# Loading the output-projection weights of quarters 1 to 3 later, and splitting the first quarter's attention rows pair by pair

## The chip, the core and the metric

The kernel runs on one core of a Trainium2 chip. The metric is the device time of one execution in microseconds, as the median of several runs; the profile comes from one execution, which has its own time.

Five engines work in parallel, each through its own queue, in order: PE (TensorE, matmuls), DVE (VectorE), ACT (ScalarE), POOL (GpSimd) and SP (SyncE, which here only issues DMA transfers). An instruction that waits holds up all behind it on its engine.

## The reference

One layer of a streaming encoder, on 2048 prompt rows and 32 sample rows of width 1024. Cut to what matters here:

```
h = rms_norm(x, g_norm1) * (1 + scale1) + shift1
q, k, v, z, xbc_raw, dt_raw = jnp.split(h @ w_in, SPLITS, axis=-1)
attn = stick_breaking(q, k, v)            # 8 heads of 64, weights from a running product of 1 - sigmoid
attn = rms_norm(attn.reshape(bsz, l, SB_WIDTH), g_attn_out)
ssm  = ssd_mixer(z, xbc_raw, dt_raw, ...) # 8 heads, chunked scan, normed
mixed = jnp.concatenate([attn, ssm], axis=-1) @ w_out
x = x + gate1 * mixed
h2 = rms_norm(x, g_norm2) * (1 + scale2) + shift2
ff = (jax.nn.silu(h2 @ w_gate) * (h2 @ w_up)) @ w_down
x = x + gate2 * ff
```

## The kernel before

All matmuls keep float32 accuracy by splitting each operand into a rounded high part and a low rest (`split`: ACT makes the high part, DVE or POOL the rest) and adding three products (`mm3`, L130 to L132). So every weight panel is loaded to a tile `wr` (1 MB), split to `wh` and `wl`, and used. `wr` has two buffers, `wh` and `wl` three each, shared by all weights.

The prompt is worked on in four quarters of 512 rows. Up to about 840 us of the profile the input projection and the state mixer run. Then come attention of quarter 0 (`attn`, a0, whole), and with it the state half of quarter 0's output projection (`Wout.ssm` of w0). `Wout.rows` loads the finished attention rows of a head pair from DRAM (`ao<-aoD`), splits them into `mH` and `mL` and sums their squares (`sq`, `t<-one,sq`); `Wout.run` does that for all four pairs, then the attention half of the product, the residual, the second norm (transposes `t<-xn`) and the store of the FFN's input. For w0 all of `run` is written behind the end of a0.

From then on two streams, written as Python generators, are mixed into one program by `merge`:

- Stream A: attention of quarters 1 to 3 with a window of near keys (`attn_w`, tiles `Kw`, `Vw`), then the far pass `far_keys` for the rows whose weight reaches past the window: seven chunks of 256 keys, each with 16 score matmuls (`fz`, from `Kf` tiles with two buffers), two sigmoids, a scan, two transposes (`t<-fb`) and 8 matmuls into `facc` (from `Vf`); and a tail in which, for quarters 1 to 3 in turn, the rows `aof` are loaded, corrected (`far`) and stored. After it come the projections (`project`) of quarters 1 and 2, of the sample, and of quarter 3. `Wout.pre` loads the state rows `mixT`, asks for the first w_out piece (`opiece`: a 1 MB load, four ACT and four DVE instructions, L114 and L115), the gate rows `gr` and the residual rows. Their pool lies where attention's tiles were, so `gr` is loaded after the far pass.
- Stream F: the FFN of the four quarters, 11 panels each. A panel is 24 gate matmuls (`pg`), 24 up (`pu`), 24 gate, 24 up, and 48 down (`py`): 144. `Pieces` asks for each panel's weights one ahead.

Each `yield n` says how long the piece just written is thought to take, in ns. `merge` writes pieces of F until they make up A's number times a ratio. F may not pass into quarter g+1 before A has finished the projection of quarter g (`yield ("need", g + 1)`, at 1536, 3120 and 4704 FFN matmuls).

What `merge` writes is not yet the order on the engines: at build time a scheduler goes through the written program, takes an instruction when by its own estimate its inputs and a buffer are there, and so can put an instruction ahead of others that were written before it. Buffers are granted in the written order. The order on each engine is fixed after that.

Of the kernel before, what the change touches and what calls it, by code (L numbers as in the profile page):

```python
# [35 lines left out]
def body(tc, nc, I, O):  # L36
    V, A, G, PE = nc.vector, nc.scalar, nc.gpsimd, nc.tensor
    ctx = ExitStack()
    with ctx:
# [15 lines left out]
        def store(dst, src):  # L55
            nc.sync.dma_start(dst, src)
# [30 lines left out]
        class Pieces:  # L87


            def __init__(self, thunks, look=1):  # L90
                self.t, self.q, self.look = list(thunks), [], look
# [5 lines left out]
            def get(self):  # L97
                self.fill(1)
                r = self.q.pop(0)
                self.fill(self.look)  # L100
                return r
# [138 lines left out]
        def sums(stat, sq, hp, n):  # L240
# [4 lines left out]
                PE.matmul(t[:m, b:b + 1], lhsT=sq[:, b * P:b * P + m], rhs=one1, start=True, stop=True)  # L245
            V.tensor_copy(stat[:m, hp, :nb], t[:m, :nb])

        def attn(g, at_, na=NA):

            aT, d1 = scan_tiles(at_, na)  # L250
            top = 2 * g + 1
            heads = {}

            todo = [(hd, kc) for hd in range(NH) for kc in range(top, -1, -1)]
            got = []

            def fetch():
                if not todo:
                    return
                hd, kc = todo.pop(0)  # L260
                hp, r0 = hd // 2, (hd % 2) * 64
                Q = None
                if kc == top:
                    Q = at_.tile([P, 512], F32R, tag="Q", name="Q", bufs=2)
                    for i in range(2):
                        load(Q[i * 64:(i + 1) * 64].bitcast(F32), QT[i, hp, r0:r0 + 64, g * 512:(g + 1) * 512])
                K = at_.tile([P, 2, 256], F32R, tag="K", name="K", bufs=3)
                c0 = kc * 256
                for i in range(2):
                    load(K[i * 64:(i + 1) * 64].bitcast(F32), KT[:, hp, r0:r0 + 64, c0:c0 + 256].rearrange("a p t -> p a t"))  # L270
                Vt = at_.tile([P, 2, P], F32R, tag="V", name="Vt", bufs=4)
                load(Vt.bitcast(F32), VS[c0:c0 + 256, hd].rearrange("(b p) a d -> p b (a d)", p=P))
                got.append((Q, K, Vt))

            def front(hd, kc):
                Q, K, Vt = got.pop(0)
                fetch()
                if kc == top:
                    heads[hd] = [Q, po.tile([P, 512], F32, tag="o", name="o")]
                Q = heads[hd][0]  # L280
                diag = kc - 2 * g
                ws = [None, None]
                for pr in (1, 0):
                    if diag == 1 and pr == 0:
                        continue
                    z = zps()
                    zv = z.rearrange("p (a b) -> p a b", a=2)
                    for i in range(2):
                        qb = pr * 2 + i
                        PE.matmul(zv[:, i, :], lhsT=Q[:, qb * P:(qb + 1) * P], rhs=K[:, 0, :], start=True, stop=False)  # L290
                        PE.matmul(zv[:, i, :], lhsT=Q[:, qb * P:(qb + 1) * P], rhs=K[:, 1, :], start=False, stop=True)
                    mask = ([[P, 2], [-1, 256]], P) if diag == pr else None
                    ws[pr] = scan(at_, aT, zv, 256, d1[pr], kc == 2 * g + pr, kc == 0, mask)
                    yield 450
                return ws, Vt

            def back(hd, kc, ws, Vt):
                o = heads[hd][1]
                r0 = (hd % 2) * 64
                diag = kc - 2 * g  # L300
                hl = []
                for kb in (1, 0):
                    q0 = max(diag * 2 + kb, 0) if diag >= 0 else 0
                    t = tps()
                    for qb in range(q0, 4):
                        PE.transpose(t[:, qb * P:(qb + 1) * P], ws[qb // 2][:, qb % 2, kb * P:(kb + 1) * P], ident)
                    hh = at_.tile([P, 512], F32R, tag="hh", name="hh", bufs=2)
                    ll = at_.tile([P, 512], F32R, tag="ll", name="ll", bufs=2)
                    c = slice(q0 * P, 512)
                    split(hh[:, c], ll[:, c], t[:, c])  # L310
                    hl.append((kb, c, hh, ll))
                    yield (4 - q0) * 109
                for kb, c, hh, ll in hl:
                    vv = Vt[:, kb, :]
                    PE.matmul(o[:, c], lhsT=vv, rhs=hh[:, c], start=(kc == top and kb == 1), stop=False, skip_group_check=True)
                    PE.matmul(o[:, c], lhsT=vv, rhs=ll[:, c], start=False, stop=(kc == 0 and kb == 0), skip_group_check=True)
                    yield (512 - c.start) / 1.2
                if kc == 0:
                    hp = hd // 2
                    if hd % 2 == 0:  # L320
                        heads["a"] = at_.tile([P, 512], F32, tag="ao", name="ao", bufs=1)
                    ao = heads["a"]
                    tmp = at_.tile([P, 512], F32, tag="P", name="otmp", bufs=2)[0:64]
                    A.activation(tmp, o[64:128, :], AF.Copy)
                    V.tensor_tensor(ao[r0:r0 + 64, :], o[0:64, :], tmp, op=ALU.add)
                    if hd % 2 == 1:
                        store(aoD[g, hp], ao)

            fetch()
            fetch()  # L330
            yield 3000
            pend = None
            for hd in range(NH):
                for kc in range(top, -1, -1):
                    ws, Vt = yield from front(hd, kc)
                    if pend is not None:
                        yield from back(*pend)
                    pend = (hd, kc, ws, Vt)
            yield from back(*pend)
# [377 lines left out]
        class Wout:  # L717


            def __init__(self, g, pool, psum):  # L720
                self.g, self.pool, self.psum = g, pool, psum
                self.t0, self.n, self.s = (g * 512, 512, 0) if g < NQ else (SEQ, DEC, 1)
                self.tb = blocks(self.n)

# [3 lines left out]
            def pre(self):  # L728

                s, t0 = self.s, self.t0  # L730
                mH, mL = mHL
                for i, t in enumerate((mH, mL if s == 0 else mH[:, :, DEC:])):
                    load(t[:, :, :self.n].bitcast(F32), mixT[i, :, :, t0:t0 + self.n].rearrange("k p t -> p k t"))
                self.pf = Pieces([lambda k=k, hf=hf, g=g: opiece(k, hf, g) for k, g in ((4, gsc), (0, gac)) for hf in range(2)])
                self.pf.fill(1)
                xsrc = I["x_prompt"][0, t0:t0 + self.n] if s == 0 else I["x_sample"][0]
                self.gr, self.x1 = [], {}
                for hf in range(2):
                    t = self.tile("gr", "gr")
                    load(t.rearrange("p (m c) -> p m c", m=4), modD[16 + hf * 4:20 + hf * 4, s].unsqueeze(0).to_broadcast([P, 4, P]))  # L740
                    self.gr.append(t)
                for b, c, m in self.tb:
                    x1 = self.tile("x1", "x1", nb=len(self.tb), w=D)
                    load(x1[:m], xsrc[c:c + m])
                    for hf in range(2):
                        self.x1[hf, b] = x1[:, hf * 512:(hf + 1) * 512]
# [27 lines left out]
            def rows(self):  # L774

                mH, mL = mHL
                if self.s == 0:
                    def get(hp):
                        ao = self.tile("ao", "ao")
                        load(ao, aoD[self.g, hp])  # L780
                        return ao

                    nxt = [get(0), get(1)]
                    yield 1500
                    for hp in range(4):
# [50 lines left out]
                    yield 450  # L836

            def run(self):
                yield from self.rows()
                nb, m0 = len(self.tb), self.tb[0][2]  # L840
                ra = sm.tile([P, 4], F32, tag="ra", name="ra", bufs=2)
                V.tensor_reduce(ra[:m0, :nb], stat[:m0, :, :nb].rearrange("p h b -> p b h"), axis=AX.X, op=ALU.add)
# [152 lines left out]
        def project(g, pool):  # L995
            w = Wout(g, pool, zps)
            w.pre()
            yield 3000
            yield from w.ssm()
            yield from w.run()  # L1000

# [597 lines left out]
        with ExitStack() as pb_:  # L1599
            mp = pb_.enter_context(tc.tile_pool(name="mp", bufs=1))  # L1600
            mHL, stat = mixed(mp)
            pw0 = ExitStack()
            w0 = Wout(0, pw0.enter_context(tc.tile_pool(name="wo0", bufs=1)), dense_ps)
            w0.pre()
            merge2(a0, w0.ssm(), R1)
            pa0.close()
            fc = px_.enter_context(tc.tile_pool(name="fc", bufs=1, side="right"))
            far_consts(fc)
# [28 lines left out]
            def streamF():  # L1637
                hT = load_h(0, fp, None)
                for g in range(NQ):
                    hT = yield from ffn(g, fp, late, hT)  # L1640

            merge(streamA(), streamF(), 1.55)


        fx = ctx.enter_context(tc.tile_pool(name="fx", bufs=1))
# [110 lines left out]
```

## Time and profile before

| | |
|---|---|
| median of 3 runs | 2942.09 us (2938.08 to 2947.04) |
| profiled execution, its time | 2940.34 us |
| its span, first to last instruction | 2938.4 us |
| PE busy | 2729.8 us, 93% of the span |
| DVE, ACT, POOL busy | 53%, 40%, 52% |
| granted PE clock, mean | 0.963 |

By stage, from the stretches of the same execution:

| stretch, us | what runs | PE busy, us | granted clock |
|---|---|---|---|
| 0 to 950 | input projection, state mixer, attention of quarter 0 | 846.95 of 950 | 0.96, then 0.83 |
| 950 to 1060 | end of quarter 0, its output projection | 72.94 of 110 | 0.75 |
| 1060 to 1300 | window attention with the FFN | 230.91 of 240 | 1.00 |
| 1300 to 1502 | far pass with the FFN, quarter 1's first products | 168.34 of 202 | 0.91 |
| 1502 to 2500 | projections with the FFN | 986.19 of 998 | 1.00 |
| 2500 to 2938.4 | the FFN's last part | 424.46 of 438.4 | 0.99 |

A busy PE is not always at its full pace, since matmuls overlap; the pace is read from the number of matmuls in a stretch. The granted clock is the share of full speed that PE was given.

### The profile page before, as it was taken

The numbers are of one execution on the slowest core, as the hardware profiler recorded it, in microseconds if no ns is written. First come the engines' busy times: TensorE is split into PE (matmuls) and PEld (weight loads), VectorE is DVE, ScalarE is ACT, GpSimd is POOL, SyncE is SP. The second block draws the span as 40 slices with busy tenths as digits, with TensorE's granted clock in tenths as the row PEclk, the third lists the DMA queues.
The fourth block names the chain that finished last, engine by engine and source line by source line (L and its number), as shares of the span: only waits on it lengthen the run. The fifth ranks groups of instructions, "written<-read, shape, count | busy, mean of one in ns | idle before, by whom it ended". The sixth has DMA issues, their size and how long they took to land.

```text
span 2938.4 us, 41844 instructions
## 1 busy us (share of the span) xinstructions
PE 2729.8 (93%) x15467; PEld 2334.2 (79%) x15467; DVE 1563.9 (53%) x2575; ACT 1186.0 (40%) x2533; POOL 1532.6 (52%) x1318
## 2 busy tenths in 40 slices
PE   6998998998978689998879999999999999999998
PEld 5988997896977578876667887777787788899997
DVE  6577586766568567874344534434434422333336
ACT  6466365555535455522224334333243422322221
POOL 4767566564654635743136655544564445544445
PEclk8999998999988789999989999999999999999999
DMA  8755653463467787837745744534733722422221
GB/s 266 219 171 153 202 177 114 119 182 106 131 175 237 193 225 196 208 116 213 199 165 180 258 135 137 152 122 155 236 127 106 230 88 92 154 87 87 86 87 66
DMA packets 415619, 466.54 MB, mean 159 GB/s; under 512 B 34191, under 2 KB 330991, under 8 KB 415406
## 3 DMA queue, kind: packets, MB, share of 16 engines
q1 hardware_dynamic: 414478, 463.61, 52.7%
q8 instruction: 124, 2.03, 0.3%
q14 instruction: 89, 0.73, 0.1%
q10 hardware_dynamic: 896, 0.14, 0.0%
q0 software_dynamic: 32, 0.03, 0.0%
HBM read 372.66 MB, written 91.04 MB: 158 GB/s over the span
## 4 chain that ended last, share of the span: by engine, by line
PE 57%; DVE 6%; DMA 5%; issue 3%; POOL 2%; ACT 2%; SPq 1%; DVEq 0%; ACTq 0%; POOLq 0%
PE pg L130 5%; PE pg L131 5%; PE pg L132 5%; PE pu L130 5%; PE pu L131 5%; PE pu L132 5%; PE py L130 5%; PE py L131 4%; PE py L132 4%; PE z L130 2%; PE z L131 2%; PE z L132 1%; PE d L131 1%; PE d L130 1%; PE d L132 1%
## 5 line engine op out<-in xcount | busy, mean ns | idle before, releaser
L60 POOL TENSOR_TENSOR wl<-wr,wh 128x512 fp32r<-128x512 f32 x752 | 1010.3, 1375 | 861.7 <-ACT wh L59 778.5
L59 ACT ACTIVATE wh<-wr 128x512 fp32r<-128x512 f32 x816 | 450.3, 620 | 512.3 <-PE py L132 128.4
L130 PE MATMUL d<-wh,hH 128*128 128x256 f32 (+2 forms) x1088 | 316.0, 291 | 18.8 <-ACT hH L59 10.9
L132 PE MATMUL d<-wh,hL 128*128 128x256 f32 (+2 forms) x1088 | 311.8, 287 | 6.7 <-POOL hL L60 6.7
L130 PE MATMUL pg<-h,wh 128*128 128x512 f32 (+1 forms) x880 | 311.3, 354 | 3.7 <-POOL aT L378 2.5
L130 PE MATMUL pu<-h,wh 128*128 128x512 f32 (+1 forms) x880 | 310.5, 353 | 1.2 <-DVE sg L952 1.2
L131 PE MATMUL d<-wl,hH 128*128 128x256 f32 (+2 forms) x1088 | 311.4, 286 | 0.0
L132 PE MATMUL pg<-h,wl 128*128 128x512 f32 (+1 forms) x880 | 310.7, 353 | 0.6 <-POOL wl L60 0.6
L131 PE MATMUL pg<-h,wh 128*128 128x512 f32 (+1 forms) x880 | 310.7, 353 | 0.0
L132 PE MATMUL pu<-h,wl 128*128 128x512 f32 (+1 forms) x880 | 310.5, 353 | 0.0
L131 PE MATMUL pu<-h,wh 128*128 128x512 f32 (+1 forms) x880 | 309.9, 352 | 0.0
L130 PE MATMUL py<-wh,aH 128*128 128x512 f32 x704 | 282.5, 401 | 7.0 <-DVE ya L983 5.0
L131 PE MATMUL py<-wl,aH 128*128 128x512 f32 x704 | 277.0, 394 | 0.0
L983 DVE TENSOR_TENSOR ya<-py,ya 128x512 f32<-128x512 f32 x288 | 190.4, 684 | 148.4 <-PE py L132 146.8
L132 PE MATMUL py<-wh,aL 128*128 128x512 f32 x704 | 265.8, 394 | 2.8 <-DVE aL L60 2.8
L952 DVE TENSOR_TENSOR sg<-pg,sg 128x512 f32<-128x512 f32 (+1 forms) x110 | 64.8, 589 | 336.8 <-ACT sg L951 336.8
L130 PEld LDWEIGHTS d<-wh,hH 128*128 128x128 f32 (+1 forms) x1088 | 207.7, 191 | 23.2 <-ACT hH L59 12.5
L132 PEld LDWEIGHTS d<-wh,hL 128*128 128x128 f32 (+1 forms) x1088 | 206.9, 190 | 8.0 <-POOL hL L60 7.2
L131 PEld LDWEIGHTS d<-wl,hH 128*128 128x128 f32 (+1 forms) x1088 | 207.3, 191 | 0.7
L130 PEld LDWEIGHTS pg<-h,wh 128*128 128x128 f32 x880 | 165.6, 188 | 28.5 <-POOL aT L378 2.7
L130 PEld LDWEIGHTS pu<-h,wh 128*128 128x128 f32 x880 | 165.5, 188 | 24.2 <-DVE sg L952 1.4
L132 PEld LDWEIGHTS pg<-h,wl 128*128 128x128 f32 x880 | 165.4, 188 | 24.1 <-POOL wl L60 1.1
(434 smaller groups left out, 5686.7 us busy)
## 6 DMA issues: line engine op xcount, KB each, us to landing
wr<-in_w_in SPq DMA_DIRECT2D x48, 1024.0 KB
wr<-in_w_gate SPq DMA_DIRECT2D x44, 1024.0 KB
wr<-in_w_up SPq DMA_DIRECT2D x44, 1024.0 KB
wr<-in_w_down SPq DMA_DIRECT2D x44, 1024.0 KB
wr<-in_w_ada SPq DMA_DIRECT2D x24, 1024.0 KB
wr<-in_w_out SPq DMA_DIRECT2D x20, 1024.0 KB
h2D<-hl SPq DMA_DIRECT2D x64, 256.0 KB
Kw<-KT SPq DMA_DIRECT2D x48, 320.0 KB
```

The source lines that it names most:

```text
L59: A.activation(h, src, AF.Copy)
L60: (eng or V).tensor_tensor(l, src, h.bitcast(F32), op=ALU.subtract)
L130: PE.matmul(out, lhsT=sh, rhs=mh, start=(i == 0), stop=False)
L131: PE.matmul(out, lhsT=sh, rhs=ml, start=False, stop=False)
L132: PE.matmul(out, lhsT=sl, rhs=mh, start=False, stop=(i == n - 1))
L952: V.tensor_tensor(sg[:, :n], pg[:, :n], sg[:, :n], op=ALU.mult)
L983: V.tensor_tensor(dst, ps[:r], dst, op=ALU.add)
```

## The change

Three edits.

1. `pre` asks for the first w_out piece only for quarter 0. For the others `project` asks for it after a yield of 3500, and the products follow after 4500 more; before it was 3000 in all.
2. For quarter 0, `rows` is written into the mix with a0: it waits until `attn` has stored a pair, loads that pair, splits it and sums its squares. `run` then skips `rows`.
3. The ratio of the two streams goes from 1.55 to 1.45. (It becomes 4.0 after quarter 1's projection, before and now.)

```
+        stored = []
...
                         store(aoD[g, hp], ao)
+                        stored.append(hp)
...
-            def __init__(self, g, pool, psum):
+            def __init__(self, g, pool, psum, alone=True):
...
-                self.pf.fill(1)
+                if self.g == 0:
+                    self.pf.fill(1)
...
+                    if self.g == 0 and not self.alone:
+                        for hp in range(4):
+                            while len(stored) <= hp:
+                                yield 200
+                            ao = get(hp)
+                            yield 1500
+                            split(mH[:, hp, :], mL[:, hp, :], ao)
+                            sq = self.tile("tm", "sq")
+                            A.activation(sq, ao, AF.Square)
+                            yield 500
+                            sums(stat, sq, hp, 512)
+                        return
...
             def run(self):
-                yield from self.rows()
+                if self.alone:
+                    yield from self.rows()
...
             w.pre()
-            yield 3000
+            yield 3500
+            w.pf.fill(1)
+            yield 4500
             yield from w.ssm()
...
-            merge2(a0, w0.ssm(), R1)
+            merge2(a0, chain(w0.ssm(), w0.rows()), R1)
...
-            merge(streamA(), streamF(), 1.55)
+            merge(streamA(), streamF(), 1.45)
```

What the scheduler makes of it, at three places. First ACT, around the splits of quarter 0's rows (`mH<-ao`) and their squares (`sq<-ao`); `wh<-wr` is the FFN's first weights, `hh<-t` and `otmp` belong to attention's last head pair. Before:

```order
L59 ACTIVATE mH<-ao 128x512 x2
L59 ACTIVATE wh<-wr 128x512
L789 ACTIVATE sq<-ao 128x512
L59 ACTIVATE wh<-wr 128x512 x2
L324 ACTIVATE otmp<-o 64x512
L59 ACTIVATE wh<-wr 128x512
L59 ACTIVATE hh<-t 128x256
L59 ACTIVATE mH<-ao 128x512
L789 ACTIVATE sq<-ao 128x512
```

Now:

```order
L59 ACTIVATE mH<-ao 128x512 x2
L59 ACTIVATE wh<-wr 128x512
L795 ACTIVATE sq<-ao 128x512
L59 ACTIVATE wh<-wr 128x512 x2
L326 ACTIVATE otmp<-o 64x512
L59 ACTIVATE wh<-wr 128x512
L59 ACTIVATE hh<-t 128x256
L59 ACTIVATE mH<-ao 128x512
L795 ACTIVATE sq<-ao 128x512
```

Only the lines of the code are others; the instructions and their order are the same.

Second PE, in the sixth of the seven far chunks, around its transposes. Before:

```order
L131 MATMUL py<-wl,aH 128x512
L132 MATMUL py<-wh,aL 128x512
L594 MATMUL t<-ident,fb 128x128 x2
L575 MATMUL fz<-Kf,Qz 128x256 x2
L130 MATMUL py<-wh,aH 128x512
L131 MATMUL py<-wl,aH 128x512
L132 MATMUL py<-wh,aL 128x512
```

Now:

```order
L605 MATMUL facc<-Vf,fl 128x512
L578 MATMUL fz<-Kf,Qz 128x256 x12
L597 MATMUL t<-ident,fb 128x128 x2
L578 MATMUL fz<-Kf,Qz 128x256 x2
L605 MATMUL facc<-Vf,fh 128x512 x2
L605 MATMUL facc<-Vf,fl 128x512 x2
L578 MATMUL fz<-Kf,Qz 128x256 x4
```

The down matmuls (`py`) that stood between the score matmuls are gone; twelve score matmuls, of which the last four belong to the seventh chunk, stand together ahead of the transposes.

Third SP, where the first two w_out loads stand among the key loads of the far pass (`Kf`, 112 in all). Before:

```order
L53 DMA Kf<-KT 64x2x256
L53 DMA wr<-in_w_out 128x4x512
L53 DMA Vf<-VS 128x512
L53 DMA Kf<-KT 64x2x256 x12
L53 DMA wr<-in_w_out 128x4x512
L53 DMA Vf<-VS 128x512 x2
L53 DMA Kf<-KT 64x2x256 x8
L53 DMA Vf<-VS 128x512 x2
L53 DMA Kf<-KT 64x2x256 x8
L53 DMA wr<-in_w_gate 128x8x256
```

Now:

```order
L53 DMA wr<-in_w_gate 128x8x256
L53 DMA Kf<-KT 64x2x256 x16
L53 DMA wr<-in_w_out 128x4x512
L53 DMA Vf<-VS 128x512 x2
L53 DMA Kf<-KT 64x2x256 x8
L53 DMA Vf<-VS 128x512 x2
L53 DMA Kf<-KT 64x2x256 x8
L53 DMA wr<-in_w_out 128x4x512
L53 DMA Vf<-VS 128x512 x2
```

The two loads stood after 68 and 80 key loads, and the gate panel after them; now they stand after 48 and 64, and the gate panel ahead of them.

More of the change, by code (lines that the diff above doesn't have):

```diff
@@ L717, in body @@
         class Wout:
-            def __init__(self, g, pool, psum):
-                self.g, self.pool, self.psum = g, pool, psum
+            def __init__(self, g, pool, psum, alone=True):
+                self.g, self.pool, self.psum, self.alone = g, pool, psum, alone
                 self.t0, self.n, self.s = (g * 512, 512, 0) if g < NQ else (SEQ, DEC, 1)
@@ L1602, in body @@
             pw0 = ExitStack()
-            w0 = Wout(0, pw0.enter_context(tc.tile_pool(name="wo0", bufs=1)), dense_ps)
+            w0 = Wout(0, pw0.enter_context(tc.tile_pool(name="wo0", bufs=1)), dense_ps, False)
             w0.pre()
-            merge2(a0, w0.ssm(), R1)
+            merge2(a0, chain(w0.ssm(), w0.rows()), R1)
             pa0.close()
```

## The prediction

> **What bounds the kernel now.** I read the page first (busy shares, slices, groups), then stretches of the span, then the order of time where PE is not full, then who waited for the tiles there.
>
> ```profile
> PE 2729.8 (93%) x15467; PEld 2334.2 (79%) x15467; DVE 1563.9 (53%) x2575; ACT 1186.0 (40%) x2533; POOL 1532.6 (52%) x1318
> PE   6998998998978689998879999999999999999998
> PEclk8999998999988789999989999999999999999999
> ```
>
> PE is the bound: 93% busy. A slice is 73.5 us; after the first, PE is at 6 or 7 only in the 12th (808 to 882 us, ahead of the change), the 14th (955 to 1028) and the 21st (1469 to 1543). The order of the work is fixed at build time and PE takes it in that order, so a change of order with the same matmuls costs or saves PE idle time and slow clock, nothing else.
>
> ```profile
> 950.00:1000.00 50.00, 36.58 (x168) 29.55 (x167) 32.45 (x42) 18.46 (x37) 31.03 (x34) 0.83 0.58 143
> 1060.00:1300.00 240.00, 230.91 (x1295) 196.59 (x1294) 191.89 (x288) 122.31 (x227) 141.48 (x138) 1.00 0.73 186
> 1300.00:1400.00 100.00, 91.32 (x424) 72.71 (x423) 40.77 (x65) 24.17 (x49) 37.11 (x28) 1.00 0.67 180
> 1450.00:1500.00 50.00, 31.01 (x93) 21.22 (x92) 19.84 (x34) 1.24 (x3) 2.54 (x3) 0.70 0.60 206
> 1500.00:1550.00 50.00, 50.00 (x230) 41.01 (x229) 24.27 (x35) 17.33 (x31) 23.91 (x19) 0.98 0.37 120
> 2400.00:2450.00 50.00, 50.00 (x216) 40.20 (x215) 16.62 (x25) 13.68 (x26) 26.14 (x20) 1.00 0.33 106
> ```
>
> (Stretch, then busy time and count of PE, PEld, DVE, ACT and POOL, granted clock, DMA share, GB/s.) Where only the FFN runs, PE is full, at 50/216 = 0.2315 us a matmul. The change touches two places where it is not: the first quarter's end (950 to 1050), and the far pass with the start of quarter 1's projection (1400 to 1500).
>
> **First quarter: nothing moves.** The code asks that pairs 0 to 2 be loaded and split during attention. The trace shows that this already happens.
>
> ```profile
> L59 ACT ACTIVATE mH<-ao x16: 613/632/633, 957.4 to 2146.0; 128x512 fp32r<-128x512 f32 x16
> L325 DVE TENSOR_TENSOR ao<-o,otmp x8: 655/680/684, 875.1 to 973.0; 64x512 f32<-64x512 f32 x8
> 973.71 0.33 SPq L56 DMA_DIRECT2D aoD<-ao  x1
> 976.25 0.33 SPq L53 DMA_DIRECT2D ao<-aoD  x1
> 979.78 0.80 PE L130 MATMUL d<-wh,mH 128*128 128x512 f32 x1 [5.33 <-ACT mH L59]
> ```
>
> The first split starts at 957.4, the last head's rows are made at 973.0: the scheduler had hoisted the loads out of the later code. The new build has the same instructions in the same order with the same waits on all five queues up to the first down panel of the FFN, beyond this stage (the first piece of order above shows ACT). The 5.33 us wait for the last pair's store and reload stays. Cost and gain: 0.
>
> **The far pass: the FFN stops one panel earlier.** All weight panels share three wh/wl buffers. Quarter 1's first two w_out pieces take two of them and keep them until its state products have run; these need the gate rows, which land only after the last store of the far pass.
>
> ```profile
> 1491.33 0.92 SPq L53 DMA_DIRECT2D gr<-modD  x2
> 1495.27 1.41 DVE L761 SCALAR_TENSOR_TENSOR tm<-z,rsS,gr 128x512 f32<-128x512 f32 x2 [6.14 <-DMA gr<-modD]
> 1496.08 0.79 PE L130 MATMUL z<-wh,mH 128*128 128x512 f32 x1 [8.00 <-DVE tm L761]
> 1504.58 2.57 ACT L114 ACTIVATE wh<-wr,cols 128x512 fp32r<-128x512 f32 x4 [36.69 <-PE z L132]
> ```
>
> Read upward: the third w_out piece waits 36.69 us for a buffer, until the products run (1496), after gr (1491 to 1495). So the FFN stops in both builds after the gate half-panel (24 matmuls) that follows those two pieces. Counting pg, pu and py in PE's order, 1176 stand ahead of the first far matmul before and 1032 now, one panel of 144 less. Between the 80th and the last of 112 fz matmuls there were 99, and to the first far matmul 123; now 2. The last two of seven chunks and the pass's tail run bare (second piece of order).
>
> What that stretch takes now:
>
> ```profile
> 1408.12 0.40 PE L575 MATMUL fz<-Kf,Qz 128*128 128x256 f32 x2
> 1448.91 0.39 ACT L580 ACTIVATE aT<-fz 128x256 f32<-128x256 f32 x1 [1.70 <-PE fz L575]
> 1449.20 0.38 ACT L581 ACTIVATE fb<-fz 128x256 f32<-128x256 f32 x1
> 1451.88 0.42 DVE L590 TENSOR_TENSOR fb<-fb,fP 128x256 f32<-128x256 f32 x1
> 1456.51 0.38 PE L594 MATMUL t<-ident,fb 128*128 128x128 f32 x2
> 1470.32 1.41 PE L642 MATMUL far<-S,OZ 128*128 128x512 f32 x4
> 1408.10:1470.30 62.20, 52.69 (x216) 40.79 (x215) 29.05 (x55) 12.70 (x26) 5.22 (x4) 0.90 0.71 205
> ```
>
> From the 80th fz (1408.12) to the first far (1470.32): 62.2 us, PE 52.7 busy. The 121 FFN matmuls that leave are worth 121 x 0.2315 = 28.0 us and run later, where PE is full. So the stretch must come down to 34.2 us to break even. What holds it up:
>
> ```profile
> 1415.49 5.35 SPq L53 DMA_DIRECT2D Kf<-KT  x8
> 1423.34 0.80 SPq L53 DMA_DIRECT2D Vf<-VS  x2
> 1447.04 0.69 PE L575 MATMUL fz<-Kf,Qz 128*128 128x256 f32 x2 [2.10 <-DMA Kf<-KT]
> 1447.00:1450.50 3.50, 3.08 (x9) 2.46 (x10) 1.16 (x2) 0.88 (x3) 3.50 (x4) 0.52 0.90 279
> ```
>
> - Two bare chunks. Each needs 16 Kf and 4 Vf issues from SP: 16 x 5.35/8 + 4 x 0.80/2 = 12.3 us. Its 24 matmuls take 5.6 us at 0.2315, twice that at half clock: less, so SP is the pace. Two chunks 24.6 us, and one landing wait of 2.10 us, because the up and down panels (1 MB each) stand in SP's queue just ahead: 26.7 us. Bounds: no wait, 24.6; a wait of 2.10 at each of the eight Kf tiles, 41.4. I take the lower part: a tile's issue outlasts its use on PE, and no panel load stands behind the sixth chunk.
> - The tail, last sigmoid to far: 1470.32 - 1448.91 = 21.4 us. Its transposes waited until 1456.51 behind gate matmuls, though fb was ready at 1452.30. Now 12 product matmuls stand there, in the bank that the sigmoids free at 1449.58; at the half clock seen after such gaps (0.52 in the row above, so 0.2315/0.52 = 0.445 us a matmul) they end at 1454.9, which saves 1.6 us: 19.8 us. Bounds: 17.2 if the transposes start at 1452.3, 21.4 if nothing is saved.
>
> Sum 26.7 + 19.8 = 46.5 us against 34.2: **+12.3 us**. Bounds 41.8 (+7.6) and 62.8 (+28.6); the upper needs every wait at its worst.
>
> The half clock came after a gap of only 2.10 us. The Trainium skill, TensorE: Matmul & The Clock Gate, "Why this matters for your kernels", says drops are avoided while idle gaps stay under about 3 us. By that rule the 12 products would run at full clock, 2.6 us shorter, and the sum would be +9.7. The row decides: I keep the half clock.
>
> **The other terms.** Ratio 1.55 to 1.45 in attention of quarters 1 to 3: 772 FFN matmuls stand ahead of the 16th fz now, 812 before. The 40 less are part of the 144. PE is 96% full there (230.91 of 240) and DVE 80%; taking 9.3 us of PE away brings DVE to 83%, still no bound: 0. From the far matmuls to the products: the same 24 far matmuls and the same store, load and gr chain, both times after 24 product matmuls: 0. The 36 products and 72 FFN matmuls that then follow fill PE as the 78 products did (50.00 of 50 in 1500 to 1550): 0. The weights' fill 3500 later and the 5000 more in all per projection spread quarters 2, 3 and the sample over more FFN work; quarter 2's last transposes stand after 2262 FFN matmuls, quarter 3's after 4002, ahead of 3120 and 4704, where the FFN first needs them: 0. One wait may go or come:
>
> ```profile
> 1600.87 0.77 PE L130 MATMUL z<-wh,mH 128*128 128x512 f32 x1 [2.38 <-DMA mH<-mixT]
>   DMA wr<-in_w_out: 2.8, 2
> ```
>
> Quarter 2's mH load was 2.38 us late; 126 FFN matmuls stand ahead of its first product now, so up to -2.4. ACT waited 2.8 us in all for w_out to land, in two places; I take 0 for both.
>
> Against the profiled execution, 2940.34 (span 2938.4): 2940.3 + 12.3 = **2952.6 us**. That execution lies 1.8 under the median of the runs, 2942.09; about 0.3% (8.8 us) is what this measurement can tell from no change.
>
> **Rivals.**
> - *Same*, 2948: the bare chunks keep the SP pace without landing waits and the tail starts early, +7.6. For it: the chain needs nothing from the FFN. Against: the two panel loads in SP's queue. 0.29.
> - *Faster*, 2932: the thinner mixture and the wider spacing let late operands come in time wherever PE now waits for them: 9.1 us in 1060 to 1300, 8.7 in 1300 to 1400, 2.4 at the mH load, 20.2 in all. All of it gone gives 12.3 - 20.2 = -7.9 on its own time, 9.7 under the median. It decides from 12.3 of the 20.2 on. For it: PE waits there for K, V and DVE results, not for other matmuls. Against: fewer matmuls also cover less. 0.13.
> - *Slower still*, 2960: the later fill. In the trace w_out cost ACT 2.8 us; four projections with a first piece late by as much as one such pair would add 8, and the sum is +20. Against it: 126 FFN matmuls, 29 us, stand ahead of quarter 2's first product. 0.08. The Trainium skill, DMA: Bandwidth & Descriptors, "Rules for kernel authors", states the rule behind it: issue a transfer early and wait for it late. The trace so far agrees little, 2.8 us in five projections.
> - My forecast, 0.50.
>
> With a part of *faster* that falls short: slower by over 0.3% 0.57; within 0.32; faster 0.11. The range takes in the *same* case, part of *faster* and most of the upper bound: 2936 to 2966; the likeliest case alone has 2948 to 2960.
>
> **What would show it.** Right: the far chunks 6 and 7 with no pg, pu or py between them, some 12 to 14 us apart, PE half idle and its clock at half for about 25 us ahead of the first far matmul; that matmul near 1450, the end some 12 us later. First quarter: same times to 1090 us. Wrong: chunks that follow each other in 8 to 9 us, or a first far matmul ahead of 1438; or attention (1060 to 1300) ending more than 12 us early for its number of matmuls.

## The result, and the profile after

| | before | changed |
|---|---|---|
| median | 2944.57 us | 2978.44 us (2976.16 to 2981.24) |
| ratio | | 1.0118, 95% interval 1.0095 to 1.0140 |
| profiled execution, span | 2938.4 us | 2979.5 us |

The change makes the kernel 34 us slower. The forecast was 12.3 us slower, 2952.6, with 2966 as the upper end: the direction was right, the size was not. Two places carry the loss. One is the far pass, which the prediction named and priced too low; the other lies 600 us later, and the prediction had it at nothing.

From the page of the changed kernel's profile, the busy line and the two lines of slices that the prediction showed of before:

```profile
PE 2740.9 (92%) x15467; PEld 2342.8 (79%) x15467; DVE 1543.0 (52%) x2575; ACT 1186.3 (40%) x2533; POOL 1532.1 (51%) x1318
PE   7998998998978599998599999999799999999998
PEclk8999998999988799999699999999899999999999
```

As many matmuls as before. A slice is 74.5 us. The 20th (1415 to 1490) has fallen to 5 tenths with a clock of 6; before, the dip there was the 21st, a 7 with a clock of 8. And the 29th (2086 to 2160) shows a 7 with a clock of 8 where before there were only nines.

The stretches that the prediction showed of before, now of the changed kernel, and two new ones: the bare stretch from the 80th fz to the first far matmul, and the new dip.

```profile
950.00:1000.00 50.00, 36.56 (x168) 29.54 (x167) 32.41 (x44) 18.14 (x37) 30.98 (x34) 0.83 0.55 142
1060.00:1300.00 240.00, 230.04 (x1285) 196.05 (x1284) 191.28 (x289) 122.82 (x228) 144.98 (x138) 0.99 0.72 187
1300.00:1400.00 100.00, 95.53 (x446) 76.85 (x445) 39.43 (x72) 24.75 (x48) 25.84 (x20) 1.00 0.72 195
1450.00:1500.00 50.00, 31.39 (x92) 20.47 (x91) 19.23 (x33) 2.83 (x6) 6.58 (x6) 0.71 0.50 179
1500.00:1550.00 50.00, 50.00 (x229) 40.80 (x227) 17.92 (x28) 16.18 (x28) 24.57 (x19) 1.00 0.37 116
1403.00:1463.60 60.60, 33.42 (x90) 22.55 (x91) 13.39 (x32) 3.87 (x11) 0.00 (x0) 0.58 0.54 145
2105.00:2145.00 40.00, 19.95 (x78) 15.54 (x79) 10.62 (x17) 7.64 (x20) 15.33 (x14) 0.79 0.87 302
```

(Stretch, then busy time and count of PE, PEld, DVE, ACT and POOL, granted clock, DMA share, GB/s.) The first five are close to those of before (in the third PE does 22 matmuls more). In the sixth PE runs 90 matmuls in 60.6 us at a clock of 0.58. In the last it is busy half the time; the kernel before, in the same 40 us:

```profile
2105.00:2145.00 40.00, 39.92 (x180) 32.11 (x179) 19.54 (x25) 15.18 (x27) 28.00 (x22) 1.00 0.53 184
```

**The far pass.** The changed kernel's order of time on PE and SP, the two bare chunks (Kf and Vf are the key and value tiles, two buffers each):

```profile
1402.87 0.48 PE L578 MATMUL fz<-Kf,Qz 128*128 128x256 f32 x2 [1.76 <-DMA Kf<-KT]
1413.37 1.88 SPq L53 DMA_DIRECT2D Kf<-KT  x3
1417.10 0.79 PE L605 MATMUL facc<-Vf,fh 128*128 128x512 f32 x1 [3.79 <-DMA Vf<-VS]
1418.35 1.45 SPq L53 DMA_DIRECT2D Vf<-VS  x2
1419.85 11.57 SPq L53 DMA_DIRECT2D Kf<-KT  x15
1424.65 0.77 PE L578 MATMUL fz<-Kf,Qz 128*128 128x256 f32 x2 [4.36 <-DMA Kf<-KT]
1444.74 0.77 PE L578 MATMUL fz<-Kf,Qz 128*128 128x256 f32 x2 [3.20 <-DMA Kf<-KT]
1463.61 0.63 PE L645 MATMUL far<-S,OZ 128*128 128x512 f32 x2
```

Read with the waits: at 1415.25 SP comes to a Vf load whose buffer is still in use. PE frees it only after 1417.10, since it waited 3.79 us itself for the Vf before. SP goes on at 1418.35, the K loads behind go out from 1419.85, and PE waits 4.36 us for them. From the 80th fz (the second of the pair at 1402.87) to the last (1445.09, the second of the pair at 1444.74) it is 42.0 us; the tail to the first far matmul takes another 18.5. What SP waited for in these 43 us (in total, times, longest):

```profile
SPq L53 <- PE facc L605: 7.3, 7, 2.2
SPq L53 <- DMA Kf<-KT: 6.6, 3, 3.5
```

The first row is V buffers that PE freed late; the second the profile puts down to landings of K loads. The two chunks in the kernel before, and now:

```profile
1408.00:1449.00 41.00, 35.01 (x156) 27.56 (x155) 18.43 (x35) 10.88 (x22) 3.26 (x3) 0.94 0.86 243
1403.00:1446.00 43.00, 19.96 (x56) 13.11 (x56) 5.41 (x16) 3.03 (x9) 0.00 (x0) 0.56 0.68 180
```

Before, the 80th to the last fz took 40.2 us with 99 FFN matmuls in between. Those are gone, and the chunks have not become shorter.

**The seam of the FFN's quarters 1 and 2.** Here quarter 1's last panel brings its residual (ya, xf) in, and the sample's projection ends. The changed kernel, in order of time:

```profile
2108.45 0.54 POOL L150 TENSOR_TENSOR rsd<-rs,mhalf 32x1 f32<-32x1 f32 x1 [3.27 <-DVE rs L149]
2110.71 0.68 PE L841 MATMUL t<-ident,xn 32*128 32x32 f32 x8
2111.24 2.26 ACT L847 ACTIVATE hx<-t,mods,A 128x32 f32<-128x32 f32 x8 [5.31 <-PE t L841]
2113.55 2.22 ACT L59 ACTIVATE wh<-wr 128x512 fp32r<-128x512 f32 x4
2114.29 6.22 POOL L60 TENSOR_TENSOR wl<-wr,wh 128x512 fp32r<-128x512 f32 x5 [5.30 <-ACT wh L59]
2120.48 1.25 POOL L941 TENSOR_TENSOR ya<-ya,xf 128x512 f32<-128x512 f32 x1
2121.76 1.74 DVE L1004 TENSOR_TENSOR ya<-ya,yt 128x512 f32<-128x512 f32 x1 [4.83 <-POOL ya L941]
2124.35 0.79 PE L130 MATMUL pg<-h,wh 128*128 128x512 f32 x1 [12.96 <-DVE yt L1003]
2143.16 0.80 PE L130 MATMUL pg<-h,wh 128*128 128x512 f32 x1 [5.71 <-DVE yt L1003]
```

A chain through five in-order queues: the sample's norm (rsd on POOL, xn on DVE, transposes t on PE, hx on ACT); ACT stands 5.31 us for the transposes with weight splits behind; POOL stands 5.30 us for those splits, with the residual's addition behind; DVE stands 4.83 us for that, with the product yt behind, which empties the accumulator bank that PE writes next; and PE stands 12.96 us for that bank.

### The profile page after: what moved, and what is told of

It is laid out like the page before. It is cut to its first block, busy times and chain, and to the rows that moved or that the text cites. A ratio compares the mean times of both kernels' runs of the same rounds, so it can differ in the third digit from the quotient of the medians.

```text
span 2979.5 us, 41835 instructions
## 1 busy us (share of the span) xinstructions
PE 2740.9 (92%) x15467; PEld 2342.8 (79%) x15467; DVE 1543.0 (52%) x2575; ACT 1186.3 (40%) x2533; POOL 1532.1 (51%) x1318
## 4 chain that ended last, share of the span: by engine, by line
PE 60%; DVE 5%; DMA 5%; POOL 2%; issue 2%; ACT 1%; SPq 1%; DVEq 0%; ACTq 0%; POOLq 0%
PE pg L130 5%; PE pg L131 5%; PE pg L132 5%; PE pu L130 5%; PE pu L132 5%; PE pu L131 5%; PE py L130 5%; PE py L131 5%; PE py L132 5%; PE z L130 2%; PE z L131 2%; PE z L132 1%; DMA Vf<-VS 1%; PE d L131 1%; PE d L130 1%
## 5 line engine op out<-in xcount | busy, mean ns | idle before, releaser
L974 DVE TENSOR_TENSOR sg<-pu,sg 128x512 f32<-128x512 f32 (+1 forms) x110 | 65.0, 591 | 253.8 <-PE pu L132 252.8
L767 POOL TENSOR_TENSOR x<-x,tm 128x512 f32<-128x512 f32 (+1 forms) x68 | 96.2, 1419 | 180.3 <-DMA x<-in_x_prompt 118.4
```

Of the source, the lines that this page charges most:

```text
L767: G.tensor_tensor(x1[:m], x1[:m], tm[:m], op=ALU.add)
L974: V.tensor_tensor(sg[:, :n], pu[:, :n], sg[:, :n], op=ALU.mult)
```

## The experiments

A profiled execution can lie some us off its program's median: 7 above it for rows_only (2951.74), 8 for far_covered_2 (2960.47), 4 below it for the kernel before (2940.34). So each run is also read by its two places. All programs have the same matmuls. Each matmul was counted at the spacing it has where PE is full, and the times at which two programs had done the same amount were compared. "Far" is what a program lost on the kernel before between before's 1240 and 1545 us, "seam" between 2049 and 2339 us; both from one execution, and uncertain by some 3 us, by the spacing that is taken. "FFN ahead" counts FFN matmuls ahead of the first far matmul and, behind the stroke, those after the 80th fz; "sample" is where its last transposes stand.

| kernel | FFN ahead | sample | far, us | seam, us | ratio to before, interval |
|---|---|---|---|---|---|
| changed | 1032/2 | 3168 | 25.6 | 19.4 | 1.0118 (1.0095 to 1.0140) |
| ratio_only | 1032/2 | 2976 | 24.4 | -4.0 | 1.0052 (1.0034 to 1.0069) |
| late_weights_only | 1176/123 | 3240 | 1.0 | 7.4 | 1.0022 (1.0008 to 1.0036) |
| rows_only | 1176/123 | 3105 | 4.0 | 0.8 | 0.9994 (0.9980 to 1.0008) |
| sample_soon | 1032/2 | 3096 | 27.1 | 4.5 | 1.0076 (1.0047 to 1.0105) |
| yields_145 | 1032/2 | 3168 | 28.6 | 18.6 | 1.0143 (1.0122 to 1.0163) |
| late_fill_145 | 1032/2 | 2976 | 27.9 | -5.1 | 1.0062 (1.0040 to 1.0085) |
| panel_back | 1152/122 | 2905 | 5.9 | -4.5 | 0.9969 (0.9957 to 0.9982) |
| far_covered | 1266/213 | 2982 | -9.5 | -6.1 | 0.9999 (0.9987 to 1.0011) |
| all_sample_early | 1032/2 | 2832 | 33.4 | 1.3 | 1.0096 (1.0071 to 1.0121) |
| all_panel_back | 1176/146 | 3168 to 3194 | -3.2 | 3.8 | 1.0024 (1.0013 to 1.0035) |
| all_both_mended | 1176/146 | 2905 | 0.3 | -1.2 | 0.9956 (0.9939 to 0.9973) |
| far_covered_2 | 1266/213 | 2832 | -3.9 | 3.6 | 1.0026 (1.0010 to 1.0042) |
| vf_other_queue | 1032/0 | 2976 | 12.4 | -4.8 | 1.0032 (1.0016 to 1.0049) |
| residual_dve | 1032/2 | 3168 | 27.1 | -1.2 | 1.0075 (1.0045 to 1.0105) |
| best_vf | 1176/144 | 2905 | -4.1 | -0.2 | 0.9960 (0.9945 to 0.9975) |

**ratio_only**, the third edit alone.

```
-            merge(streamA(), streamF(), 1.55)
+            merge(streamA(), streamF(), 1.45)
```

> Before with the third edit alone (ratio 1.45). The changed kernel lost time at two places: 20 us by the end of the far pass, and 20 more at the seam of the FFN's quarters 1 and 2 (2105 to 2145 us), where a gate matmul waited 12.96 and then 5.71 us. Theory, two stalls with two causes: the ratio makes the first. 1032 FFN matmuls stand ahead of the first far matmul here, as in the changed kernel, and the sample's last transposes stand after 2976 of them, well ahead of the seam at 3120. So 18 to 22 us slower than before, some 2965 us, all of it between 1400 and 1510, and no PE wait over 3 us at the seam. Rival, one cause: the seam's stall follows from the panel that is missing, since all later FFN work then stands otherwise against the projections: 35 to 41 slower, some 2980. By the step of the prediction (bare stretch 46.5 us) it would be 12 slower, 2957.

2959.87 us, 16 slower. Far pass and seam, of this kernel:

```profile
1405.50:1464.30 58.80, 33.23 (x91) 22.82 (x91) 14.30 (x35) 3.87 (x11) 0.00 (x0) 0.57 0.50 141
2095.00:2160.00 65.00, 65.00 (x289) 52.73 (x288) 32.81 (x42) 22.10 (x39) 45.76 (x33) 1.00 0.71 240
```

The bare stretch is that of the changed kernel, and PE is full at the seam. The ratio alone makes the first loss and not the second.

**late_weights_only**, the first edit alone.

```
             w.pre()
-            yield 3000
+            yield 3500
+            w.pf.fill(1)
+            yield 4500
```

(and in pre, fill(1) for quarter 0 alone.)

> Before with the first edit alone (first w_out piece asked for after a yield of 3500, products after 4500 more; ratio 1.55). The order of the far pass on PE is that of before (1176 FFN matmuls ahead of the first far matmul, 123 behind the 80th fz); the sample's last transposes stand after 3240 FFN matmuls instead of 3105, behind the seam at 3120. Theory, two causes: no loss in the far pass, 15 to 22 us lost at the seam; some 2962 us. Rival, one cause (the panel): no loss, 2945 us within 9. Rival, late weights themselves: waits of ACT for in_w_out ahead of each of four projections, some 3 us each, spread over 1500 to 2400 us and not at the seam.

2950.00 us: 6 slower, and where the theory had it, but less than its 15 to 22. With the sample at 3240 the seam cost 7.4 us.

**sample_soon**, the whole change with the sample's yields cut.

```
-            yield 3500
+            k = 3 / 8 if g == NQ else 1
+            yield 3500 * k
             w.pf.fill(1)
-            yield 4500
+            yield 4500 * k
```

> The changed kernel with the sample's two yields cut to 3/8 (1312 and 1688, 3000 in all, as before); quarters 1 to 3 keep 3500 and 4500. The sample's last transposes stand after 3096 FFN matmuls, ahead of the seam, instead of 3168. Theory, two causes: the seam's stall goes, the far pass stays 20 us slower; some 2962 us. Rival (the seam's stall comes from the missing panel, or from quarter 2's or 3's later weights): nothing changes, 2978 us.

2966.70 us, 12 less than the change and near the theory's 2962. At the seam 4.5 us are left, with one wait of 2.81.

**rows_only**, the second edit alone (code as in the change).

> Before with the second edit alone (the first quarter's rows inside its attention). Every engine has the order of before up to the FFN's first down panel. Theory: same as before, 2945 us within 9, with the same 5.3 us wait of PE for the last pair's split. Rival (the edit lets the last pair come earlier or holds up an engine ahead of it): a change of more than 9 us, seen between 950 and 1060 us.

2944.28 us against 2943.85: nothing, as expected.

**yields_145** and **late_fill_145** part the first edit's halves, both at the ratio 1.45: the longer yield with the early load, and the late load with the old 3000 in all.

```
yields_145:     -            yield 3000
                +            yield 8000
late_fill_145:  -            yield 3000
                +            yield 1300
                +            w.pf.fill(1)
                +            yield 1700
```

(late_fill_145, and the programs below with a yield of 10000 or 20000 that start from the kernel before, also have the line in pre.)

> Before with the ratio 1.45 and a yield of 8000 ahead of each projection's products, but the first w_out piece asked for at once, as before. The sample's last transposes stand after 3168 FFN matmuls, as in the changed kernel. The ratio alone gave +16 us (1.0052), the whole change +34 (1.0118). Theory: it is the longer yield that pushes the sample's end onto the seam of quarters 1 and 2, so this is as slow as the whole change, some 2976 us, with a PE wait of over 8 us on yt near 2110. Rival (the later asking for w_out costs the rest): 2960 us, no such wait.

> Before with the ratio 1.45 and the first w_out piece asked for after a yield of 1300, the products after 1700 more (3000 in all, as before). PE's order is that of the ratio alone, with the sample's last transposes after 2976 FFN matmuls. Theory: asking later costs nothing, so as the ratio alone, some 2960 us, and no long wait at the seam. Rival (the later asking costs the rest): some 2972 us, with ACT waiting for in_w_out.

2984.39 and 2960.71 us, both as the theory had it. The longer yield makes the second loss; asking for the weights later costs nothing (1.0062 beside 1.0052 for the ratio alone, the intervals overlap; no wait of ACT for w_out shows in late_fill_145). Of yields_145 at the seam:

```profile
2128.43 0.79 PE L130 MATMUL pg<-h,wh 128*128 128x512 f32 x1 [12.95 <-DVE yt L986]
2095.00:2160.00 65.00, 45.42 (x181) 35.00 (x180) 30.07 (x41) 18.00 (x39) 27.86 (x22) 0.84 0.82 284
```

**panel_back** gives the far pass its panel again at the ratio 1.45: F gets written ahead of quarter 1's first w_out piece, so its panel gets the buffers.

```
-            yield 3000
+            yield 10000 if g == 1 else 1300
+            w.pf.fill(1)
+            yield 1700
...
-                        yield ("ratio", 4.0)
+                        yield ("ratio", 3.6)
...
-            merge(streamA(), streamF(), 1.55)
+            merge(streamA(), streamF(), 1.45)
```

> The ratio 1.45 in attention, but quarter 1 asks for its first w_out piece only after a yield of 10000, so that an FFN panel's weights get their buffers ahead of it: 1152 FFN matmuls stand ahead of the first far matmul (1032 with the ratio alone, 1176 before), 122 of them behind the 80th fz (2; 123). Quarter 1's last transposes stand after 1428, the sample's after 2905 (a ratio of 3.6 instead of 4.0 behind quarter 1). Theory: the far pass loses only for want of those matmuls, so the time is that of before, 2944 us within 9, and PE waits in 1400 to 1465 are those of before. Rival (the ratio costs 15 us in other ways: less FFN in attention, operands later): some 2958 us.

2935.48 us: the far loss shrinks from 24 to 6, and the whole is 9 us faster than before. So the lost panel, not the ratio as such, is what the far pass paid for.

**far_covered**: as panel_back, but with the ratio 1.55 kept and the yield 20000 in place of 10000.

> Ratio 1.55 as before, quarter 1's first w_out piece asked for after 20000: 1266 FFN matmuls ahead of the first far matmul, 213 of them behind the 80th fz, and 66 more among the far matmuls. The sample's last transposes stand after 2982 (ratio 3.6 behind quarter 1). Quarter 1's projection ends later, its last transposes after 1584 FFN matmuls, just as quarter 0 of the FFN ends. Theory (PE loses time in the far pass for want of FFN matmuls): of the 17 us that PE is idle in 1440 to 1485 in the kernel before, and the half clock beside them, some 10 to 15 us go; up to 10 may come back where the FFN's quarter 1 must wait for the projection; some 2936 us. Rival (the far pass is bound by its loads, which the FFN's weights delay): no gain there, 2944 to 2955.

2944.54 us, no gain. In the far pass the theory was right: PE is busy 96.07 of 110 us there, and was 85.01 before.

```profile
1400.00:1510.00 110.00, 96.07 (x417) 75.79 (x416) 48.00 (x83) 22.14 (x43) 20.82 (x16) 0.94 0.66 198
1653.88 0.80 PE L130 MATMUL pg<-h,wh 128*128 128x512 f32 x1 [18.40 <-DMA h<-h2D]
```

But quarter 1's projection ended after 1584 FFN matmuls, and at the seam of quarters 0 and 1 PE waited 18.40 us (and 3.71 more) for its result.

**all_sample_early**, **all_panel_back**, **all_both_mended** keep all three edits and mend one place, the other, or both.

```
all_sample_early:  -                        yield ("ratio", 4.0)
                   +                        yield ("ratio", 3.2)
all_panel_back:    -            yield 3500
                   +            yield 10000 if g == 1 else 3500
all_both_mended:   both
```

> The whole change, with the ratio behind quarter 1's projection 3.2 instead of 4.0; no yield is touched. The sample's last transposes stand after 2832 FFN matmuls instead of 3168, the far pass is that of the change (1032 ahead of the first far matmul). Theory (where the sample's end falls against the seam at 3120 sets the second stall, and nothing else): no wait over 3 us near the seam, the far pass as slow as in the change, so about 16 us slower than before, 2961 us. Rival (the longer yields cost by themselves, wherever the sample ends): 2975 to 2980.

> The whole change, but quarter 1 asks for its first w_out piece after 10000 instead of 3500: 1176 FFN matmuls ahead of the first far matmul, 146 of them behind the 80th fz. The sample's last transposes stay behind the seam, after 3168 to 3194. Theory (two causes that add up): the far pass loses nothing now, the seam's stall stays: 12 to 20 us slower than before, some 2960 us. Rival (the seam's stall needs the missing panel): as before, 2945.

> The whole change with both mends: quarter 1's first w_out piece after 10000, ratio 3.2 behind quarter 1. 1176 FFN matmuls ahead of the first far matmul, the sample's last transposes after 2905. Theory (the two places are the whole loss): the time of before or a few us less, 2935 to 2948. Rival (something else in the change costs too): 2955 or more.

2972.19, 2949.55 and 2928.77 us. The seam of all_sample_early is clean (1.3 us) with the long yields kept, so place decides there; but the total fell by 6 us and not 17, because its "far" is 33.4, with the same order on PE. Seven programs with these bare chunks have 24.4 to 33.4 us there. Of the 8 us that this one loses beyond the change only 2 lie in the two chunks (44.1 us for 42.0); it already waited longer for V and K tiles ahead of them (3.51 us at 1341.81, where the change waited 1.58 at 1337.09). Why is open. all_panel_back lost nothing in the far pass and only 3.8 us at the seam, and 9.0 ahead of it, with a wait of 6.32 us at the transposes of the sample's rows (the profile names a weight load that was issued just ahead of those rows): less than expected. With both mended the kernel is 13 us faster than before by the ratio, 0.9956 (15 by the medians), and some 50 faster than the change. Neither place has a gain to show (0.3 and -1.2), so the lead arises elsewhere; that was not followed. Its two places:

```profile
1400.00:1510.00 110.00, 85.99 (x326) 64.97 (x325) 46.80 (x80) 15.97 (x32) 13.86 (x10) 0.83 0.65 199
2095.00:2160.00 65.00, 65.00 (x297) 53.30 (x296) 25.11 (x38) 26.25 (x51) 36.24 (x27) 1.00 0.53 180
```

**far_covered_2** covers the far pass too, but hurries quarter 1 with a ratio of 0.8 behind its first piece.

```
-            yield 3000
+            yield 20000 if g == 1 else 1300
+            w.pf.fill(1)
+            if g == 1:
+                yield ("ratio", 0.8)
+            yield 1700
...
-                        yield ("ratio", 4.0)
+                        yield ("ratio", 3.6)
```

> Before with quarter 1's first w_out piece asked for after 20000, and then a ratio of 0.8 instead of 1.55 until quarter 1's projection is written (3.6 behind it). As in the kernel whose far pass was covered, 1266 FFN matmuls stand ahead of the first far matmul, 213 behind the 80th fz, with 42 more among the far matmuls; but quarter 1's last transposes stand after 1443 FFN matmuls, not 1584, ahead of the seam at 1536. In that kernel PE was 23 us ahead of before when the far pass ended, and lost 18.40 and 3.71 us at that seam. Theory: the gain stays, 15 to 22 us faster than before, some 2926 us. Rival (the stall only moves into quarter 1's products, which have little FFN work beside them now): 2935 to 2945.

2952.49 us: the rival. The stall moved once more, to quarter 2's first products:

```profile
1635.72 0.80 PE L130 MATMUL z<-wh,mH 128*128 128x512 f32 x1 [14.66 <-DVE tm L762]
```

With little FFN work left beside quarters 1 and 2, PE waited there for quarter 2's gate rows (gr, issued only at 1631.0).

**vf_other_queue**, ratio 1.45 alone with the V loads on ACT's queue.

```
-                    load(Vs.bitcast(F32), ...)
+                    nc.scalar.dma_start(Vs.bitcast(F32), ...)
```

> The ratio 1.45 alone, with the far pass's V loads (Vf) issued from ACT's queue instead of SP's; the FFN stops after 1032 matmuls as with the ratio alone, none behind the 80th fz. With the ratio alone the 80th to the last fz took 40.7 us there (1405.5 to 1446.2), and the whole was 16 us slower than before. Theory (round trips through one queue: a V load waits on SP for its buffer, which PE frees late, and holds up the next K tiles): the two chunks take 28 to 32 us, the whole some 2950 us. Rival (the bytes: 3 MB a chunk, at the 180 GB/s of that stretch 17 us a chunk, whatever the queue): 38 to 42 us, some 2960 us.

2954.00 us, 1.0032 beside 1.0052 for the ratio alone; the intervals overlap a little. The 80th to the last fz took 33.7 us (1407.0 to 1440.7), 7 less than the 40.7 of ratio_only: between the two, nearer to the round trip. The stretch to the first far matmul, then SP's longest wait in total within the two chunks, here and (last row) in ratio_only:

```profile
1407.00:1459.80 52.80, 32.22 (x90) 22.46 (x89) 15.09 (x35) 3.87 (x11) 0.00 (x0) 0.61 0.65 176
SPq L53 <- PE fz L575: 6.8, 7, 1.8
SPq L53 <- PE facc L602: 8.3, 7, 2.2
```

SP no longer waits for V buffers (facc), and the loads moved faster (176 GB/s, 141 in ratio_only's stretch), so in ratio_only the bytes were not the limit. Whether they limit the 33.7 us is open: the expectation's own 17 us a chunk makes 34 for two. The kernel before moved 243 GB/s in its two chunks, but with 1 MB weight loads among them.

**residual_dve**, the whole change with one addition moved.

```
-                    G.tensor_tensor(dst[:m], dst[:m], xl_[i][:m], op=ALU.add)
+                    V.tensor_tensor(dst[:m], dst[:m], xl_[i][:m], op=ALU.add)
```

> The whole change, with the residual's second addition (ya + xf) on DVE instead of POOL; FFN and sample stand as in the change on PE (the sample's last transposes after 3168). In the change PE waited 12.96 and 5.71 us at the seam for yt, behind an addition that POOL did only at 2120.48, after five weight splits that waited for ACT. Theory (order on POOL): the first wait falls below 4 us, 8 to 14 us faster than the change, some 2966 us. Rival (xf lands late): both waits stay, 2978 us.

2967.23 us, 11 less than the change (1.0075 beside 1.0118; the intervals just touch). Both long waits are gone; the longest PE wait from 2000 to 2200 is 1.32 us.

```profile
2105.00:2145.00 40.00, 38.42 (x168) 30.32 (x169) 24.93 (x36) 15.75 (x34) 20.24 (x16) 1.00 1.01 354
2120.35 10.16 POOL L60 TENSOR_TENSOR wl<-wr,wh 128x512 fp32r<-128x512 f32 x8 [5.70 <-ACT wh L59]
```

POOL still stands 5.70 us for ACT's splits; but the addition is no longer behind it. The seam alone gained 20 us and the kernel only 11, and part of the rest shows at the next seam, where the moved addition now holds up DVE, and DVE holds up PE (the longest wait of the change there is 1.57 us):

```profile
2533.66 1.27 DVE L941 TENSOR_TENSOR ya<-ya,xf 128x512 f32<-128x512 f32 x1 [2.86 <-DMA xf<-x1D]
2535.58 0.79 PE L130 MATMUL py<-wh,aH 128*128 128x512 f32 x1 [4.17 <-DVE sg L969]
```

**best_vf**: all_both_mended with the V loads on ACT's queue.

> The kernel with both places mended (2928.8 us, 0.9956 of before), with Vf issued from ACT's queue. Its far chunks have FFN work beside them, 144 matmuls behind the 80th fz. By the round trip theory PE's waits there (2.26 and 2.59 us, and those between) shrink: 2 to 6 us faster, some 2925 us. By the bytes, or if an ACT that issues loads comes late to its sigmoids and splits: the same or slower, 2929 to 2935.

2931.98 us, 0.9960 beside 0.9956: no gain, though the two chunks took 41.1 us for 44.5. With FFN work beside the chunks their round trip does not show in the time.

## Why the prediction was right or wrong, point by point

**First quarter, nothing moves: right.** rows_only has the time of before. In the changed kernel the last pair's wait is still there, 5.31 us for 5.33:

```profile
981.33 0.80 PE L130 MATMUL d<-wh,mH 128*128 128x512 f32 x1 [5.31 <-ACT mH L59]
```

**The FFN stops a panel early and two chunks run bare: right in place and cause, too small.** The prediction did not part the w_out edits from the ratio; ratio_only shows that the ratio alone does it, and panel_back and all_panel_back that the panel in the order is what counts. The mis-sized term is the bare chunks: 26.7 us predicted, 42.0 measured. The tail was predicted at 19.8 and took 18.5. (With the last sigmoid as the border, as the prediction has it, 42.5 and 18.1.) So it is 60.5 us instead of 46.5 against the break-even of 34.2: the first far matmul was forecast near 1450 and came at 1463.61, 26 us behind break-even.

The step that failed is "SP is the pace": the chunks were to fall to what SP needs to issue their loads, 12.3 us each. They did not fall at all. In every program with the V loads on SP's queue they took 40.2 to 44.9 us, bare or with FFN matmuls beside them, so the FFN's matmuls had cost the chunks no time that shows, and nearly their whole worth of 28.0 us was lost with them. The upper bound, "a wait of 2.10 at each of the eight Kf tiles, 41.4", came out near in value, in part by luck: there were seven waits over 1 us, 1.37 to 4.36 long, 19.5 in all, and two of them were for V tiles. It was rejected because "a tile's issue outlasts its use on PE". That compares issue and use and leaves out the landing and the freeing: with two buffers and one queue, SP waits for PE, and PE for what SP issues after. vf_other_queue took 7 us away by moving the V loads alone. The rest, 33.7 us against the prediction's 24.6 of issue, was not parted further; more buffers were not tried.

**The clock.** Half clock was forecast for some 25 us; over the 60 us of the bare stretch the mean was 0.58, and three pieces of it, 51 us together, ran at 0.50. The twelve products in the tail ran at 0.44 us each, as forecast (1446.26 to 1451.54), and the last transposes came the 1.6 us sooner that were forecast. The first slow matmul came after a wait of 3.84 us. But the clock was back at full for a while and then fell again, with no wait over 1.48 us around that point:

```profile
1404.40:1435.00 30.60, 15.31 (x42) 10.63 (x42) 4.78 (x14) 1.56 (x5) 0.00 (x0) 0.50 0.67 168
1435.10:1438.40 3.30, 1.47 (x4) 0.59 (x4) 0.00 (x0) 0.00 (x0) 0.00 (x0) 1.00 0.67 208
1438.60:1452.10 13.50, 8.09 (x20) 5.67 (x20) 1.91 (x4) 0.66 (x2) 0.00 (x0) 0.50 0.51 146
1431.57 0.77 PE L578 MATMUL fz<-Kf,Qz 128*128 128x256 f32 x2 [1.48 <-DMA Kf<-KT]
1436.43 0.50 PE L605 MATMUL facc<-Vf,fh 128*128 128x512 f32 x1 [1.37 <-DMA Vf<-VS]
```

The rule of the Trainium skill (TensorE: Matmul & The Clock Gate, "Why this matters for your kernels") is that drops are avoided while idle gaps stay under some 3 us. This fall speaks against it, as the prediction's gap of 2.10 us did.

**"Ratio ... 0" and "from the far matmuls to the products: 0": right.** Attention lost nothing to 1240 us (-0.2, within the uncertainty). The products waited for gr as before:

```profile
1487.65 1.41 DVE L765 SCALAR_TENSOR_TENSOR tm<-z,rsS,gr 128x512 f32<-128x512 f32 x2 [5.72 <-DMA gr<-modD]
1488.46 0.79 PE L130 MATMUL z<-wh,mH 128*128 128x512 f32 x1 [7.27 <-DVE tm L765]
```

The 2.38 us wait for quarter 2's mH load, which the prediction let go or stay, is gone. About 5 us of the changed kernel's far loss came back by 2049. ratio_only, which has the far loss without the other, is 16 us slower in the median; that is within the forecast's bounds of 7.6 to 28.6, but 4 us that it gains at the seam are in it.

**"Spread quarters 2, 3 and the sample over more FFN work: 0": wrong, and the larger failure.** The step asked only whether quarters 2 and 3 end ahead of the FFN counts at which the FFN needs them (3120, 4704). The sample is needed much later, so its place was not asked about at all. It stood at 3105 before and at 2976 with the ratio alone; the longer yields put it at 3168, into the FFN's own seam at 3120, and the chain shown above cost 19.4 us. (Quarter 3's last transposes stand after 4134 FFN matmuls, not 4002; that is still ahead of 4704.) Three experiments show the cause: it is the yields (yields_145 against late_fill_145), by the place and not by their length (all_sample_early), through the addition's place on POOL (residual_dve). The price depends on the exact place: 3.6 us or less at 2832 to 2982, 4.5 at 3096, nothing at 3105 (before itself), 18.6 to 19.4 at 3168 with the addition on POOL, 3.8 where the transposes are spread from 3168 to 3194, 7.4 at 3240. So the chain is shown, but no rule for the price.

**The rivals.** *Slower still* came nearest in time (2960) with the wrong mechanism: late weights cost nothing (in the changed kernel ACT waited 2.6 us for w_out, 2.8 before). *Faster* was possible: with both places mended the same three edits give 2928.8 us, below that rival's 2932. How much of that the edits bring and how much the mends was not parted; panel_back, without the longer yields of quarters 2 and 3, has 9 of the 13 us.

## What to carry to other kernels

Where a scheduler fixes the order, a small number in a planner (a ratio, a yield) moves the order in jumps: a whole panel of 144 matmuls here for 0.1 of the ratio. Read each seam of the background stream in the new order, and ask what else now ends there, also work that nobody needs soon: on in-order engines its waits stop whatever stands behind them. And price a stretch that loses its cover by the round trip (buffer freed, issued, landed, used), not by the longer of issue and use.

## What was not expected of the hardware

A stretch that two queues share moved more than with one: with K loads on SP's queue and V loads on ACT's, the bare stretch moved 176 GB/s where one queue gave 141, and the chunks took 33.7 us in place of 40.7; SP had stood 8.3 us for V buffers in them, and then no longer did. And the granted clock stayed at 0.57 to 0.58 on average through 60 us in which PE was busy more than half of the time, with waits of 1 to 4 us.
